# Down projection of the last two blocks: plain tiles before, quads of seven half-size products after

## The chip, the cores and the metric

One Trainium2 chip, one of its cores. The metric is the device time of one execution in microseconds (us), median of several runs. The engines are TensorE (PE, with its weight loads PEld), VectorE (DVE), ScalarE (ACT), GpSimd (POOL) and SyncE (SP, whose queue issues all DMAs here).

## The reference

One step of a one-layer hybrid decoder (width 1024) on 2048 prompt tokens and 8x8 sample tokens, 2112 columns in all. Four recurrent mixers (RWKV-7, GLA, gated DeltaNet, Mamba-2) work side by side on the projected input; then comes the part that the change touches, the channel mixer and the final norm:

```python
x = x + gt1 * (y @ w_out)
h = rmsnorm(x, norm2_w) * (1 + sc2) + sh2
x = x + gt2 * (jnp.square(jax.nn.relu(h @ w_up)) @ w_down)   # 1024 -> 4096 -> 1024
y = rmsnorm(x, final_norm_w)
```
All in float32. The kernel holds activations transposed: features on the 128 partitions, tokens on the free axis.

## The kernel before, in words

**Exactness.** Each float32 operand is split into a rounded part `hi` and the rest `lo`, and `mm3` (L111 to 119) forms a product by three matmuls (hi*hi, hi*lo, lo*hi; lines L117, L118, L119) for each slice of 128 of the inner dimension. A weight tile of 128x512 is therefore loaded (`wr`), cast on ACT (`wh`) and subtracted on DVE or POOL (`wl`): `wload` (L92), or `split` (L361), which takes turns between POOL and DVE when no engine is named.

**Stages.** The input projection runs in four passes, with the mixers beside it. Then the tokens go through the channel mixer in blocks, `F_BLOCKS` (L26): two small ones (352 and 360 columns) and two of two tiles of 350 each, the "last two blocks". `F_out` (L321) transposes the mixers' output, multiplies by w_out and writes the residual x to DRAM (`x2`); it is called for the next block in the last step of a small block (L2200 to 2206).

**Up projection of the last two blocks.** It goes by quads: two row tiles of 128 by two column tiles of 350, the inner dimension in two halves of 512. Such a 2x2 product by blocks is made with seven products instead of eight. `forms_x` (L368) makes the seven right factors from the normed input once per block (x2 and x3, in the slots x0 to x13 and z0 to z13; a slot is 128x1400, and a factor takes two, hi and lo). `forms_w` (L415) makes the seven left factors for each quad: four loads of 128x512, three sums on POOL and one on DVE (L428), seven splits (L366). `quad` (L449) runs the seven products, twelve matmuls each, over three PSUM banks, and after each product `read` takes the bank's running sum. `up_quad` (L463) adds, applies relu and square, and stores four hidden tiles of 128x350 to DRAM (L2246, `fd<-r`). Block 2 alone goes through 12 of the 16 quads (`SOLO`), F_out of block 3's second tile stands behind the first of them, then four quads serve both blocks, and then 12 serve block 3 alone. The steps of block 3's forms_x are emitted one per quad in between.

**Down projection of the last two blocks.** Both together, as four column tiles, in eight steps of 512 hidden features. `hidden` (L509) reloads a step's four hidden tiles (128x1400) from DRAM through four raw slots and splits them; `F_down2` (L520) goes over eight row tiles of 128 and four column tiles, twelve matmuls each, and adds each result times its gate into the residual (`gated_add`, L314). The last step runs in three parts (two tiles, one, one), each with the ending `F_end2` (L531): sum of squares, rstd, scaling (L545), store.

**What sets the order.** The program is emitted in the order told; a planner then orders each engine's instructions by priority and by its own estimate of times, and keeps that order fixed. Each engine, and SP's queue of DMAs, works in order. A tile with a tag has a fixed number of buffers, and a new one waits until the old one's last reader is done.

Of the kernel before, what the change touches and what calls it, by code (L numbers as in the profile page):

```python
# [28 lines left out]
WR, WH, WL = 4, 3, 3  # L29
# [7 lines left out]
class Dense:  # L37
    def __init__(self, es, tc, io):
# [6 lines left out]
        self.uid = self.lo_i = self.mod_i = 0  # L45
        self.held = self.aux = self.w_dma = self.xalloc = self.dsh = None
# [321 lines left out]
    def forms_x(self, bi, rs, slot, out, tmp):  # L368
# [10 lines left out]
        for k in range(4):  # L379
            q = {}  # L380
            for name, kk, t0, r in (("12", k, tb, rb), ("11", k, ta, ra), ("22", k + 4, tb, rb), ("21", k + 4, ta, ra)):
                t = q[name] = tmp(k, False)[:, :n]
                self.xget(t, self.x2, kk, t0, n)
                nc.vector.scalar_tensor_tensor(out=t, in0=t, scalar=self.A2[:, kk, 0:1], in1=r[:, :n], op0=ALU.mult, op1=ALU.mult)

            def sub(a, b, eng, o=None):
                o = tmp(k, True)[:, :n] if o is None else o
                eng.tensor_tensor(out=o, in0=a, in1=b, op=ALU.subtract)
                return o
# [10 lines left out]
            t1 = sub(q["12"], q["11"], nc.gpsimd)  # L400
            put(0, q["11"], s0)
            put(2, q["21"], s1)
            yield
            u = sub(q["22"], t1, nc.vector)
# [10 lines left out]
    def forms_w(self, srcs, wide):  # L415

        nc = self.nc
        ws = lambda: self.sb.tile([128, 512], F32, tag="ws", name=self.n("ws"), bufs=4)[:, :wide]
        raw = {}
        for i, h in ((0, 0), (1, 0), (1, 1), (0, 1)):  # L420
            t = ws() if (i, h) == (1, 0) else self.wp.tile([128, 512], F32, tag="wr", name=self.n("wr"), bufs=WR)[:, :wide]
            nc.sync.dma_start(t, srcs[i][:, h * wide : h * wide + wide])
            raw[i, h] = t
        a11, a12, a21, a22 = raw[0, 0], raw[0, 1], raw[1, 0], raw[1, 1]

        def comb(a, b, op, out=None):
            o = ws() if out is None else out
            (nc.gpsimd if out is None else nc.vector).tensor_tensor(out=o, in0=a, in1=b, op=op)  # L428
            return o
# [12 lines left out]
        s4 = comb(a12, s2, ALU.subtract)  # L442
        yield parts(a12, nc.vector)
        yield parts(s3, nc.gpsimd)
# [4 lines left out]
    def quad(self, srcs, wide, blocks, read, alt=0):  # L449


        ps = {}
        for i, w in enumerate(self.forms_w(srcs, wide)):
            bank, first = (0, 1, 0, 1, 2, 1, 2)[i], i in (0, 1, 4)
            for b, n, xs in blocks:
                if first:
                    ps[b, bank] = self.psum("de"[(b + alt) % 2])[:, :n]
                p = ps[b, bank]
                hi, lo = xs[i]
                self.mm3(p, w, [(hi[:, k], lo[:, k]) for k in range(wide // 128)], first, True, skip_group_check=True)  # L460
                read(b, i, p)

    def up_quad(self, pair, blocks, tmp, out):  # L463

        nc = self.nc
        held = {}

        def read(b, i, p):
            n = p.shape[1]
            t = lambda tag: tmp(b, tag)[:, :n]  # L470
            if i == 0:
                s = held[b, "s"] = t("s")
                nc.scalar.copy(s, p)
                return
            if i in (1, 3):
                u = held[b, i] = t("u" if i == 1 else "v")
                nc.vector.tensor_tensor(out=u, in0=p, in1=held[b, "s"], op=ALU.add)  # L477
                return
            r = t("r")
            if i == 2:  # L480
                nc.scalar.activation(r, p, AF.Relu)
            else:
                nc.vector.tensor_tensor(out=r, in0=p, in1=held[b, {4: 3, 5: "s", 6: 1}[i]], op=ALU.add)
                nc.scalar.activation(r, r, AF.Relu)
            nc.scalar.activation(r, r, AF.Square)
            row, col = {2: (0, 0), 4: (1, 1), 5: (1, 0), 6: (0, 1)}[i]
            out(2 * pair + row, 2 * b + col, r)

        self.quad([self.io["w_up"][2 * pair + i] for i in range(2)], 512, blocks, read, pair % 2 if len(blocks) == 1 else 0)
# [19 lines left out]
    def hidden(self, f_d, cc, take, raws, parts):  # L509

        f = []
        for j in range(4):
            raw = take(raws)
            self.nc.sync.dma_start(raw.bitcast(F32), f_d[cc * 4 + j])
            hi, lo = take(parts), take(parts)
            self.split(hi, lo, raw.bitcast(F32))
            f.append((hi, lo))
        return f

    def F_down2(self, tiles, f, acc, cc):  # L520

        for c2 in range(4):
            w = self.wload(self.io["w_down"][cc, c2])
            for ci in range(2):
                ct = c2 * 2 + ci
                for i, (o, n) in enumerate(tiles):
                    ps = self.psum("de"[i % 2])[:, :n]
                    self.mm3(ps, w[ci], [(fh[:, o : o + n], fl[:, o : o + n]) for fh, fl in f])
                    self.gated_add(acc[ct][:, o : o + n], ps, 40, ct, 0, n)

    def F_end2(self, acc, t0, o, n):  # L531

        nc = self.nc
        s = self.d2("ssum", 2)
        for ct in range(KT):
            self.sumsq(s[:, :n], acc[ct][:, o : o + n], ct == 0)
        r = self.rstd_bc(s, n)
        tail = t0 + n == NT
        for ct in range(KT):
            a = acc[ct][:, o : o + n]  # L540
# [1495 lines left out]
D2_BUFS = 6  # L2036
SOLO = 12
# [22 lines left out]
def build(tc, io):  # L2060
    nc = tc.nc
    with ExitStack() as es:
# [129 lines left out]
        pl = es.enter_context(tc.tile_pool(name="left", bufs=1, side="left", reuse_waits="tile"))  # L2192
        hs = first["hs"]
        for bi in range(SMALL):
# [5 lines left out]
            for cc in range(8):  # L2200
                f = K.F_up(bi, hs, lambda j: (f0[:, 0, j], f0[:, 1, j]), cc)
                if cc == 7:
                    rs = K.F_out(bi + 1, yload, ("a0", "a1"))
                    if final:
                        rs2 = K.F_out(bi + 2, yload, ("a0", "a1"), slice(0, 1), salloc=lambda: pl.tile([128, BIG], F32, tag="ssum", name=K.n("ssum"), bufs=2))
# [8 lines left out]
        W2 = 4 * BIG  # L2214
        slots = {}

        def slot(pool, tag):
            slots[tag] = pool.tile([128, W2], F32R, tag=tag, name=K.n("sl"), bufs=1)
            return slots[tag]

        def y_act(tags, n):
            t = [slot(pr, tag).rearrange("p (k n) -> p k n", k=4) for tag in tags]
            return [HalfTiles(t[:2]), HalfTiles(t[2:])]

        def yall(t0, m):
            t = slot(pr, yslots.pop(0)).bitcast(F32)[:, :1024]
            yget(t, t0, m, slice(0, 1024))
            return t

        yslots = ["z6", "z7", "z8"]  # L2230
        x2, x3 = [], []
        small = lambda tag, bufs: pl.tile([128, BIG], F32, tag=tag, name=K.n(tag), bufs=bufs)
        first_x = lambda k, second: (small("s2", 3) if second else pl.tile([128, 512], F32, tag="ws", name=K.n("xw"), bufs=4)) if k % 2 else K.d2()
        for _ in K.forms_x(two[0], rs, lambda i: slot(pl, f"x{i}"), x2, first_x):
            pass
# [6 lines left out]
        f_d = [K.dram.tile([128, W2], F32, name=f"fd{i}") for i in range(32)]  # L2242
        T0 = F_BLOCKS[two[0]][0][0]
        K.xalloc = lambda: pr.tile([128, BIG], F32, tag="r2", name=K.n("r2"), bufs=3)
        tmp = lambda b, tag: K.xalloc() if tag == "r" else K.d2() if b else small("s2", 3)
        fout = lambda ct, q, r: nc.sync.dma_start(f_d[ct][:, q * BIG : q * BIG + BIG], r)  # L2246
        late = list(range(16 - SOLO, 16))
        for i, p in enumerate(late):
            K.up_quad(p, [(0, BIG, x2)], tmp, fout)
            if i == 0:  # L2250
                rs2 += K.F_out(two[1], yload, ["z0", "z2", "z3", "z4"], slice(1, 2), act=y_act, yall=yall)
                mod = K.forms_x(two[1], rs2, lambda i: slot(pr, f"z{i}"), x3, lambda k, second: K.d2())
            else:
                next(mod)
        for _ in mod:
            pass
        for p in range(16 - SOLO):
            K.up_quad(p, [(0, BIG, x2), (1, BIG, x3)], tmp, fout)
        for p in late:
            K.up_quad(p, [(1, BIG, x3)], tmp, fout)  # L2260
        raws = [f"x{i}" for i in range(4)]
        free = [f"x{i}" for i in range(4, 12)] + [f"z{i}" for i in range(6, 14)]
        acc = []
# [137 lines left out]
```

## Time and profile before

| | us |
|---|---|
| median of 3 runs | 3460.47 |
| lowest and highest | 3449.18 and 3468.5 |
| the profiled execution | 3459.12 |
| its span, first to last instruction | 3457.2 |
| TensorE busy in the span | 3250.1 |
| up stage of the last two blocks | about 2410 to 2944 |
| down stage of the last two blocks | about 2944 to 3441 |

The profile is of one execution. Its page gives busy times by engine, 40 equal slices of the span, DMA rates and groups of instructions by source line ("L119"). Further answers from the trace give the busy times in chosen stretches of time, waits with what ended them, and single instructions in order of time. Matmuls are pipelined: a matmul's shown duration (about 325 ns for 350 columns) is about twice the distance between two of them. PEclk is the share of TensorE's clock that was granted.

### The profile page before, as it was taken

To read this page: it belongs to the slowest core of one execution; us is meant where nothing else is said; L and a number is where in the kernel's file an instruction comes from. 1 tells how busy PE (TensorE), PEld (TensorE's weight loads), DVE (VectorE), ACT (ScalarE), POOL (GpSimd) and SP (SyncE) were. 2 spreads that over 40 slices of the span, in tenths; PEclk is the share of its full clock that TensorE was granted. 3 is DMA by queue.
4 is the path that set the end of the run, shared out by engine and by line. 5 is a ranking of instruction groups with operands and counts; after the bars stand their busy time and mean duration, and the time that the engine had idled before them with its cause. 6 is when DMAs were issued, how large, how long until landed. Compare 5 with 4: busy or idle time off the path is not lost. (4 is left out here: it accounts for less than half of the span.)

```text
span 3457.2 us, 62414 instructions
## 1 busy us (share of the span) xinstructions
PE 3250.1 (94%) x22902; PEld 2966.7 (86%) x22902; DVE 2280.3 (66%) x4728; ACT 1472.2 (43%) x3054; POOL 1390.2 (40%) x1290
## 2 busy tenths in 40 slices
PE   8999999899999998999989999987789999999997
PEld 5779887898998887988878988877689999999997
DVE  3437555956767778879889869867484355445446
ACT  3443423434344454454454554444355566111113
POOL 2333334524335346346346346245375365212112
PEclk9999999899999999999988999988899999999999
DMA  9863334423235564343343333354444455322213
GB/s 307 257 184 114 91 96 133 131 83 111 93 96 132 145 141 137 104 119 101 114 136 121 98 117 96 119 162 156 147 128 125 133 168 168 119 69 93 75 34 122
DMA packets 350395, 438.61 MB, mean 127 GB/s; under 512 B 100627, under 2 KB 228395, under 8 KB 350089
## 3 DMA queue, kind: packets, MB, share of 16 engines
q1 hardware_dynamic: 350088, 434.63, 41.4%
q8 instruction: 180, 2.95, 0.4%
q14 instruction: 127, 1.03, 0.1%
HBM read 346.75 MB, written 87.74 MB: 126 GB/s over the span
## 5 line engine op out<-in xcount | busy, mean ns | idle before, releaser
L102 POOL TENSOR_TENSOR wl<-wr,wh 128x512 fp32r<-128x512 f32 x344 | 476.1, 1385 | 1105.7 <-ACT wh L100 989.5
L119 PE MATMUL psd<-a,wl 128*128 128x360 f32 (+3 forms) x2368 | 805.1, 341 | 33.1 <-DVE wl L102 27.0
L117 PE MATMUL psd<-a,wh 128*128 128x360 f32 (+3 forms) x2368 | 801.0, 339 | 7.8 <-ACT wh L100 3.9
L118 PE MATMUL psd<-a,wh 128*128 128x360 f32 (+3 forms) x2368 | 801.9, 339 | 5.6 <-DVE a L257 2.5
L100 ACT CAST wh<-wr 128x512 fp32r<-128x512 f32 x688 | 422.1, 617 | 875.7 <-PE psd L118 423.7
L119 PEld LDWEIGHTS psd<-a,wl 128*128 128x128 f32 x2368 | 463.5, 196 | 75.1 <-DVE wl L102 34.7
L117 PEld LDWEIGHTS psd<-a,wh 128*128 128x128 f32 x2368 | 463.6, 196 | 33.3 <-issue 9.8
L118 PEld LDWEIGHTS psd<-a,wh 128*128 128x128 f32 x2368 | 463.6, 196 | 22.5 <-issue 10.2
L102 DVE TENSOR_TENSOR wl<-wr,wh 128x512 fp32r<-128x512 f32 x344 | 282.4, 821 | 152.2 <-ACT wh L100 139.4
L117 PE MATMUL psd<-sl,wh 128*128 128x350 f32 x992 | 325.0, 328 | 15.3 <-DVE sl L314 3.9
L117 PE MATMUL pse<-sl,wh 128*128 128x350 f32 x992 | 323.6, 326 | 8.1 <-DVE s L477 6.2
L119 PE MATMUL pse<-sl,wl 128*128 128x350 f32 x992 | 321.8, 326 | 1.7 <-DVE wl L366 0.6
L118 PE MATMUL psd<-sl,wh 128*128 128x350 f32 x992 | 323.2, 326 | 0.0
L118 PE MATMUL pse<-sl,wh 128*128 128x350 f32 x992 | 321.4, 324 | 0.0
L119 PE MATMUL psd<-sl,wl 128*128 128x350 f32 x992 | 321.1, 325 | 0.0
L117 PEld LDWEIGHTS psd<-sl,wh 128*128 128x128 f32 x992 | 189.2, 191 | 17.5 <-issue 8.8
L117 PEld LDWEIGHTS pse<-sl,wh 128*128 128x128 f32 x992 | 188.0, 190 | 9.7 <-ACT wh L362 6.2
L871 DVE SCALAR_TENSOR_TENSOR t<-u,cw,t 128x256 f32<-128x256 f32 x288 | 188.9, 691 | 4.9 <-ACT t L867 3.9
L119 PEld LDWEIGHTS pse<-sl,wl 128*128 128x128 f32 x992 | 187.7, 189 | 3.1 <-DVE wl L366 1.2
L118 PEld LDWEIGHTS psd<-sl,wh 128*128 128x128 f32 x992 | 190.0, 192 | 0.0
L119 PEld LDWEIGHTS psd<-sl,wl 128*128 128x128 f32 x992 | 189.3, 191 | 0.6 <-DVE wl L366 0.3
L118 PEld LDWEIGHTS pse<-sl,wh 128*128 128x128 f32 x992 | 188.6, 190 | 0.1
(630 smaller groups left out, 6327.0 us busy)
## 6 DMA issues: line engine op xcount, KB each, us to landing
wr<-w_in SPq DMA_DIRECT2D x256, 256.0 KB
wr<-w_up SPq DMA_DIRECT2D x212, 256.0 KB
wr<-w_down SPq DMA_DIRECT2D x208, 256.0 KB
ada<-ada_w SPq DMA_DIRECT2D x96, 256.0 KB
wr<-w_out SPq DMA_DIRECT2D x96, 256.0 KB
u<-uo SPq DMA_DIRECT2D x128, 180.0 KB
fd<-r SPq DMA_DIRECT2D x128, 175.0 KB
sl<-fd SPq DMA_DIRECT2D x32, 700.0 KB
```

The costliest lines, as they stand in the source:

```text
L100: nc.scalar.copy(hi, raw)
L102: self.lo_eng[self.lo_i % len(self.lo_eng)].tensor_tensor(out=lo, in0=raw, in1=hi.bitcast(F32), op=ALU.subtract)
L117: nc.tensor.matmul(ps, lhsT=lh, rhs=xh, start=first and i == 0, stop=False, **kw)
L118: nc.tensor.matmul(ps, lhsT=lh, rhs=xl, start=False, stop=False, **kw)
L119: nc.tensor.matmul(ps, lhsT=ll, rhs=xh, start=False, stop=last and i == len(ks) - 1, **kw)
L871: nc.vector.scalar_tensor_tensor(out=y[:, q], in0=uv[:, q, i : i + n], scalar=w(i), in1=y[:, q], op0=ALU.mult, op1=ALU.add)
```

## The change

The down projection of each of the last two blocks goes by quads too: 2 blocks, in each 4 steps of 1024 hidden features (two halves of 512), in each 4 pairs of row tiles. The seven right factors of a step, sums and differences of hidden tiles, are made in the up stage by `up_quad` and stored to DRAM in place of the four hidden tiles (28 factors per block, 128x1400 each). `form_f` loads a factor through one of two raw slots and splits it in four pieces of 350; the first step's seven are formed during block 3's up quads 5 to 11, a later step's two in the third quad and five in the fourth quad of the step before. `down_quad` adds each product into the residual, with product 0 summed in a tile of its own (`e0`) until the last step. The down stage may put two of five weight parts into slots of its own (`wmore`), so that five are held rather than three.

With it come: each up quad serves one block (16 + 16 quads); in `forms_w` the sum s2 moves from POOL to DVE and is made in place; `forms_x` makes t1 in place and takes all its tiles from one tag with five buffers (`D2_BUFS` 6 to 5), for block 2 where odd steps had other tags; three of the four F_out tiles of the last blocks load rows of 1024 columns at once (one before); F_out of block 3's second tile stands behind three up quads (`OUT3_AT`); the sums of squares are taken as each row tile is finished, and `F_end2` runs once per column tile at the end of each block.

```diff
         def parts(x, eng=None):
-            hi = self.wp.tile([128, 512], F32R, tag="wh", name=self.n("wh"), bufs=WH)[:, :wide]
-            lo = self.wp.tile([128, 512], F32R, tag="wl", name=self.n("wl"), bufs=WL)[:, :wide]
+            self.part_i += 1
+            if self.wmore is not None and self.part_i % 5 in (1, 3):
+                t = self.wmore()
+                hi, lo = t[:, 0:512], t[:, 512:1024]
+            else:
+                hi = self.wp.tile([128, 512], F32R, tag="wh", name=self.n("wh"), bufs=WH)
+                lo = self.wp.tile([128, 512], F32R, tag="wl", name=self.n("wl"), bufs=WL)
             self.split(hi, lo, x, eng)
             return hi, lo
 
         yield parts(a11, nc.vector)
-        s1 = comb(a21, a22, ALU.add)
-        s2 = comb(s1, a11, ALU.subtract)
+        s1 = comb(ws(), a21, a22, ALU.add)
+        s3 = comb(a21, a11, a21, ALU.subtract, nc.vector)
+        s2 = comb(a11, s1, a11, ALU.subtract, nc.vector)
         yield parts(s2, nc.gpsimd)
-        s3 = comb(a11, a21, ALU.subtract, a21)
-        s4 = comb(a12, s2, ALU.subtract)
         yield parts(a12, nc.vector)
+        s4 = comb(a12, a12, s2, ALU.subtract)
         yield parts(s3, nc.gpsimd)
         yield parts(s1, nc.vector)
         yield parts(a22, nc.gpsimd)
         yield parts(s4, nc.vector)
...
+    def up_quad(self, src, xs, n, alt, tmp, out):
...
+            else:
+                add(t["u2"], p, t["u2"])
+                act(t["u2"])
+                add(new("t1"), t["u2"], t["r2"], nc.vector, ALU.subtract)
+                out(4, t["t1"])
+                add(new("t2"), t["v2"], t["t1"], nc.vector, ALU.subtract)
+                out(1, t["t2"])
+                add(t["u2"], t["v2"], t["u2"], nc.gpsimd, ALU.subtract)
+                out(3, t["u2"])
+                add(new("t4"), t["s2"], t["t2"], nc.vector, ALU.subtract)
+                out(5, t["t4"])
...
+    def form_f(self, f_d, raw, part):
+
+        hi, lo = part(), part()
+        self.nc.sync.dma_start(raw, f_d)
+        h = raw.shape[1] // 4
+        for o in range(0, 4 * h, h):
+            self.split(hi[:, o : o + h], lo[:, o : o + h], raw[:, o : o + h])
+        return [x.rearrange("p (k n) -> p k n", k=4) for x in (hi, lo)]
+
+    def down_quad(self, src, xs, n, alt, p, acc, e0, first, last, between):
...
+        def gated(row, col, x):
+            a = acc[row, col]
+            nc.vector.scalar_tensor_tensor(out=a, in0=x, scalar=self.mod[:, 40 + 2 * p + row, 0:1], in1=a, op0=ALU.mult, op1=ALU.add)
...
+        def add(i, ps):
+            if i == 0:
                 if first:
+                    nc.scalar.copy(e0, ps)
+                else:
+                    nc.vector.tensor_tensor(out=e0, in0=ps, in1=e0, op=ALU.add)
+                if last:
+                    for row, col in ((0, 1), (1, 0), (1, 1)):
+                        gated(row, col, e0)
                 return
+            gated(*{1: (0, 1), 2: (0, 0), 3: (1, 1), 4: (1, 1), 5: (1, 0), 6: (0, 1)}[i], ps)
...
+        parts = [f"x{i}" for i in range(10)] + [f"z{i}" for i in range(8)]
+        raws = ["x10", "x11"]
+        more = ["z8", "z9"]
+        pairs = ["x12", "x13", "z10", "z11", "z12", "z13", "x12", "x13"]
...
+        mod, nxt = None, []
+        for b in range(2):
+            for p in range(16):
+                c, k = p // 4, p % 4
+                K.up_quad(lambda i, h: io["w_up"][8 * c + 4 * i + k][:, h * 512 : h * 512 + 512], (x2, x3)[b], BIG, p % 2, utmp,
+                          lambda i, t: nc.sync.dma_start(f_d[b][c][i][:, k * BIG : k * BIG + BIG], t))
+                if b == 0 and p == OUT3_AT:
+                    rs2 += K.F_out(two[1], yload, ["z0", "z2", "z3", "z4"], slice(1, 2), act=y_act, yall=yall("z", (6, 7, 8)))
+                    mod = K.forms_x(two[1], rs2, lambda i: slot(f"z{i}"), x3, lambda k: K.d2())
+                elif mod:
+                    next(mod, None)
+                if b == 1 and 5 <= p < 12:
+                    nxt.append(K.form_f(f_d[0][0][len(nxt)], take(raws).bitcast(F32), lambda: take(parts)))
...
+            for c in range(4):
+                cur, nxt = nxt, []
+                at = (4 * b + c + 1) // 4, (c + 1) % 4
+                for p in range(4):
+                    def between(i):
+                        if at[0] < 2 and ((p == 2 and i < 2) or (p == 3 and 1 <= i < 6)):
+                            nxt.append(K.form_f(f_d[at[0]][at[1]][len(nxt)], take(raws).bitcast(F32), lambda: take(parts)))
+
+                    K.down_quad(lambda i, h: io["w_down"][2 * c + h, p][:, i * 512 : i * 512 + 512], cur, BIG, p % 2, p, acc[p], e0[p], c == 0, c == 3, between)
+                    if c == 3:
+                        for row in range(2):
+                            for col in range(2):
+                                K.sumsq(sums[col][:, :BIG], acc[p][row, col], p == row == 0)
+            for col, (t0, n) in enumerate(tiles2):
+                K.F_end2([acc[ct // 2][ct % 2, col] for ct in range(KT)], sums[col], t0, n, b == 1)
```

More of the change, by code (lines that the diff above doesn't have):

```diff
@@ L447, in forms_w, with quad @@
         yield parts(s4, nc.vector)
-    def quad(self, srcs, wide, blocks, read, alt=0):
+    def quad(self, src, xs, n, alt, read):
         ps = {}
-        for i, w in enumerate(self.forms_w(srcs, wide)):
+        for i, w in enumerate(self.forms_w(src)):
             bank, first = (0, 1, 0, 1, 2, 1, 2)[i], i in (0, 1, 4)
-            for b, n, xs in blocks:
-                if first:
[L457 to L473, printed above, removed]
-                return
[L475 to L489, printed above, removed]
+            if first:
+                ps[bank] = self.psum("de"[alt])[:, :n]
@@ L507, in F_up, with F_end2 @@
         return f
[L509 to L531, printed above, removed]
+    def F_end2(self, acc, s, t0, n, tail):
         nc = self.nc
-        s = self.d2("ssum", 2)
+        r = self.rstd_bc(s, n)
         for ct in range(KT):
[L536 to L540, printed above, removed]
+            a = acc[ct]
             if tail and ct in (2, 5):
@@ L2035 @@
 MOD_AT = 26
-D2_BUFS = 6
-SOLO = 12
+OUT3_AT = 2
+D2_BUFS = 5
 SMALL = sum(len(b) == 1 for b in F_BLOCKS)
@@ L2192, in build, with yall, load @@
         pl = es.enter_context(tc.tile_pool(name="left", bufs=1, side="left", reuse_waits="tile"))
+        W2 = 4 * BIG
+        slot = lambda tag: (pl if tag[0] == "x" else pr).tile([128, W2], F32R, tag=tag, name=K.n("sl"), bufs=1)
+        small = lambda tag, bufs: pl.tile([128, BIG], F32, tag=tag, name=K.n(tag), bufs=bufs)
+        def yall(side, free):
+            free = iter(free)
+            def load(t0, m):
+                t = slot(f"{side}{next(free)}").bitcast(F32)[:, :1024]
+                yget(t, t0, m, slice(0, 1024))
+                return t
+            return load
         hs = first["hs"]
@@ L2213, in build @@
         two = (SMALL, SMALL + 1)
[L2214 to L2219, printed above, removed]
+        UT = dict(s2=2, u2=2, v2=1, r2=1, t1=1, t2=1, t4=1)
+        utmp = lambda tag: (pl if tag in ("s2", "u2") else pr).tile([128, BIG], F32, tag=tag, name=K.n(tag), bufs=UT[tag])
         def y_act(tags, n):
-            t = [slot(pr, tag).rearrange("p (k n) -> p k n", k=4) for tag in tags]
+            t = [slot(tag).rearrange("p (k n) -> p k n", k=4) for tag in tags]
             return [HalfTiles(t[:2]), HalfTiles(t[2:])]
[L2225 to L2230, printed above, removed]
         x2, x3 = [], []
-        small = lambda tag, bufs: pl.tile([128, BIG], F32, tag=tag, name=K.n(tag), bufs=bufs)
-        first_x = lambda k, second: (small("s2", 3) if second else pl.tile([128, 512], F32, tag="ws", name=K.n("xw"), bufs=4)) if k % 2 else K.d2()
-        for _ in K.forms_x(two[0], rs, lambda i: slot(pl, f"x{i}"), x2, first_x):
+        for _ in K.forms_x(two[0], rs, lambda i: slot(f"x{i}"), x2, lambda k: K.d2()):
             pass
@@ L2241, in build @@
         K.phase(pl, BIG, D2_BUFS, None, lo)
[L2242 to L2263, printed above, removed]
-        for ct, tag in enumerate(["x12", "x13"] + [f"z{i}" for i in range(6)]):
-            t = slot(pl if tag[0] == "x" else pr, tag).bitcast(F32)
-            nc.sync.dma_start(t, K.x2[:, ct, T0:])
-            acc.append(t)
-        turn = {id(raws): 0, id(free): 0}
+        K.xalloc = K.d2
+        f_d = [[[K.dram.tile([128, W2], F32, name=f"fd{b}_{i}_{c}") for i in range(7)] for c in range(4)] for b in range(2)]
+        parts = [f"x{i}" for i in range(10)] + [f"z{i}" for i in range(8)]
+        raws = ["x10", "x11"]
+        more = ["z8", "z9"]
+        pairs = ["x12", "x13", "z10", "z11", "z12", "z13", "x12", "x13"]
+        e0s = ["s2", "s2", "u2", "u2", "v2", "r2", "t1", "t2"]
+        turn = {id(parts): 0, id(raws): 0, id(more): 0}
         def take(tags):
@@ L2272, in take @@
             turn[id(tags)] += 1
-            return slot(pl if tag[0] == "x" else pr, tag)
-        tiles4 = [(i * BIG, BIG) for i in range(4)]
-        f = K.hidden(f_d, 0, take, raws, free)
-        for cc in range(8):
-            cur = f
-            if cc < 7:
-                f = K.hidden(f_d, cc + 1, take, raws, free)
-                K.F_down2(tiles4, cur, acc, cc)
-        for part in (tiles4[:2], tiles4[2:3], tiles4[3:]):
-            K.F_down2(part, cur, acc, 7)
-            for o, n in part:
-                K.F_end2(acc, T0 + o, o, n)
+            return slot(tag)
@@ new lines, in build @@
+        for b in range(2):
+            tiles2 = F_BLOCKS[two[b]]
+            acc, e0 = [], []
+            for p in range(4):
+                t = slot(pairs[4 * b + p]).bitcast(F32).rearrange("p (q n) -> p q n", q=4)
+                a = {}
+                for q in range(4):
+                    row, col = q // 2, q % 2
+                    a[row, col] = t[:, q]
+                    nc.sync.dma_start(t[:, q], K.x2[:, 2 * p + row, tiles2[col][0] : tiles2[col][0] + BIG])
+                acc.append(a)
+                e0.append(utmp(e0s[4 * b + p])[:, :BIG])
+            sums = [K.d2("ssum", 2) for _ in range(2)]
+            K.wmore = lambda: take(more)
+            for c in range(4):
+                cur, nxt = nxt, []
+                at = (4 * b + c + 1) // 4, (c + 1) % 4
+                for p in range(4):
+                    def between(i):
[8 more added lines that the diff above has]
+                K.F_end2([acc[ct // 2][ct % 2, col] for ct in range(KT)], sums[col], t0, n, b == 1)
```

75 lines of the change are left out of this document (56 added, 19 removed).

## The prediction

> **What bounds the kernel now.** I read the page's first part, a table of stages for the whole core, and the same table for one matmul line, since a mean over all stages would hide where TensorE has gaps.
>
> ```profile
> PE 3250.1 (94%) x22902; PEld 2966.7 (86%) x22902; DVE 2280.3 (66%) x4728; ACT 1472.2 (43%) x3054; POOL 1390.2 (40%) x1290
> ```
> ```profile
> core 0: us, PE busy (x) PEld busy (x) DVE busy (x) ACT busy (x) POOL busy (x), PEclk, DMA share, GB/s
> 2410.00:2460.00 50.00, 29.00 (x145) 25.85 (x144) 21.21 (x32) 14.57 (x29) 10.47 (x8) 0.69 0.37 122
> 2500.00:2560.00 60.00, 44.78 (x238) 42.47 (x237) 57.68 (x71) 34.39 (x72) 42.59 (x32) 0.89 0.39 115
> 2560.00:2672.00 112.00, 112.00 (x697) 111.69 (x696) 58.06 (x82) 69.12 (x133) 68.45 (x51) 1.00 0.44 133
> 2782.00:2944.00 162.00, 161.34 (x1005) 161.09 (x1004) 88.28 (x122) 101.88 (x190) 97.53 (x69) 1.00 0.50 164
> 2944.00:3395.00 451.00, 451.00 (x2800) 451.00 (x2799) 206.37 (x282) 72.41 (x94) 93.89 (x44) 1.00 0.22 74
> ```
> ```profile
> 2410.00:2460.00 50.00, 12.78 (x36) 7.81 (x36) 0.69 0.37 122
> 2500.00:2560.00 60.00, 26.42 (x78) 16.29 (x78) 0.89 0.39 115
> 3395.00:3441.40 46.40, 25.36 (x76) 14.81 (x76) 0.96 0.42 136
> 3441.40:3457.20 15.80, 0.00 (x0) 0.00 (x0) 0.66 0.47 166
> ```
> From 2560 to 3395 us TensorE has no gap and the full clock: up stage until 2944, then down. There 451/2800 = 0.161 us passes per matmul of 350 columns, and only fewer matmuls or new gaps can move the time. Elsewhere it has gaps: the second table is L119, one matmul in three, so 2410 to 2460 holds 3x36 = 108 of them, 17.4 us of work in 50, and 2500 to 2560 234, 37.7 in 60.
>
> In that window VectorE (DVE) is busy 57.7 of 60. Why shows in the timeline:
>
> ```profile
> 2541.84 1.57 POOL L428 TENSOR_TENSOR ws<-ws,wr 128x512 f32<-128x512 f32 x1
> 2542.18 1.78 DVE L366 TENSOR_TENSOR wl<-ws,wh 128x512 fp32r<-128x512 f32 x1
> 2543.37 1.38 POOL L366 TENSOR_TENSOR sl<-d,sl 128x350 fp32r<-128x350 f32 x1
> 2543.89 1.25 DVE L397 SCALAR_TENSOR_TENSOR sl<-d,dsh,sl 128x350 fp32r<-128x350 f32 x1
> ```
> ```profile
> L366 POOL TENSOR_TENSOR wl<-ws,wh x56: 1279/1292/1657, 2413.9 to 2925.6; 128x512 fp32r<-128x512 f32 x56
> L366 DVE TENSOR_TENSOR wl<-ws,wh x56: 673/693/2748, 2418.5 to 2931.7; 128x512 fp32r<-128x512 f32 x56
> ```
> ```profile
> 2514.27 0.57 DVE L384 SCALAR_TENSOR_TENSOR d<-d,A,rstd 128x350 f32<-128x350 f32 x1
> 2519.00 0.92 POOL L366 TENSOR_TENSOR sl<-d,sl 128x350 fp32r<-128x350 f32 x1
> 2526.14 0.51 DVE L366 TENSOR_TENSOR sl<-d,sl 128x350 fp32r<-128x350 f32 x1
> ```
> ```profile
> L483 DVE TENSOR_TENSOR r<-psd,s x30: 504/523/525, 2429.9 to 2772.6; 128x350 f32<-128x350 f32 x30
> ```
> A DVE subtraction of 512 takes 0.68 us undisturbed; behind a GpSimd (POOL) one it took 1.78 and ended 0.55 us after it; the next POOL one then ended 0.79 us after DVE's. They take turns. L483, which reads PSUM, never exceeds 0.525. So DVE operations with both inputs in SBUF share one resource, "the pair", with POOL's. What can it carry? The first and last of twelve DVE and six POOL groups in 2500 to 2560:
>
> ```profile
> L397 DVE SCALAR_TENSOR_TENSOR sl<-d,mod,sl 128x350 fp32r<-128x350 f32 x16 | 15.9, 997 | 0.2 <-ACT sl L396 0.2
> ...
> L477 DVE TENSOR_TENSOR s<-psd,s 128x350 f32<-128x350 f32 x2 | 1.0, 510 | 0.0
> ```
> ```profile
> L388 POOL TENSOR_TENSOR d<-d,d 128x350 f32<-128x350 f32 x12 | 14.5, 1214 | 4.4 <-DVE sl L397 2.3 <-DVE d L384 2.1
> ...
> L366 POOL TENSOR_TENSOR sl<-d,sl 128x350 fp32r<-128x350 f32 x3 | 3.4, 1131 | 0.0
> ```
> All groups together: POOL 17 of 512 and 15 of 350; DVE 14 of 512, 35 scalar and 8 plain ones of 350, and 14 that read PSUM. By the undisturbed durations the pair's share is 17x1.28 + 15x0.92 + 14x0.68 + 35x0.57 + 8x0.51 = 69.1 us, done in 60: pair work costs 0.87 of its undisturbed sum.
>
> The Trainium skill, "SBUF — State Buffer", section "Who interferes with whom", says the loser of this pair blocks for the whole instruction. Read literally, the factor is 1.0, the window would have needed 69 us, and the sum below would be some 40 us higher; the trace has the blocking, with 0.87.
>
> **The change, part by part.** The sum goes against the profiled execution, 3459.1 us (span 3457.2), 1.4 below the median 3460.5.
>
> *Fewer matmuls.* Down before: 8 steps x 8 row tiles x 4 column tiles x 12 = 3072. After: 2 blocks x 4 x 4 quads of 7 products x 12 = 2688. 384x0.161 = **-61.8 us**.
>
> *The end.* The last step ran in three parts, each with its own ending: 3395 to 3441.4 holds 3x76 = 228 matmuls, 36.7 us, so 9.7 were lost. One part remains; I take 8 back. After the last matmul stand 15.8 us of squares, rstd, scaling and stores; both column tiles now end there: between 0 and 8x0.57 = 4.6 more, I take 2. Together **-6**.
>
> *Pair work of one weight quad.* After: POOL 3 subtractions and 2 sums, DVE 4 and 2, all of 512: 5x1.28 + 6x0.68 = 10.5, x0.87 = 9.1 us beside 84 matmuls, 13.5 us. (Before, up stage: 6 and 5, 9.6 us, and 2782 to 2944 ran without gaps.)
>
> *Up stage.* The four quads that served both blocks become eight; their preparation hides like the others'. Each quad gains three DVE and one POOL subtraction of 350, (3x0.51+0.92)x0.87 = 2.1: 11.2 of 13.5. Seven factors are formed in block 1's quads; each costs two POOL and two DVE pieces, (2x0.92+2x0.51)x0.87 = 2.5 us, and two of the seven must wait until z0 to z3 are free, at the end. The other five exceed the 2.3 us of slack by little: 0 to 9 us, I take 5. Block 1's own inputs (forms_x) already cost 60-37.7 = 22 us in 2500 to 2560; with the fuller pair I add 5 (0 to 15). Block 0's inputs now use five buffers for five tiles per step, where odd steps had buffers of their own, so each of four steps waits for its loads (0.7 MB at the page's highest rate, 307 GB/s, 2.3 us): +8 (0 to 15). Against this, F_out of the last tile moves behind two more quads:
>
> ```profile
> PE pst L337 <- DMA sl<-yd: 15.9, 2, 11.5
> ```
> Those 15.9 us of waiting get 27 us of cover, if SyncE (SP) issues the loads early: -15 (-20 to 0). SP's queue also takes seven factor stores per quad for four, behind which weight loads stand; the page's rate has room:
>
> ```profile
> GB/s 307 257 184 114 91 96 133 131 83 111 93 96 132 145 141 137 104 119 101 114 136 121 98 117 96 119 162 156 147 128 125 133 168 168 119 69 93 75 34 122
> ```
> Per quad 1 MB of weights and 1.2 MB of stores in 13.5 us are 167 GB/s. Up stage together **+3** (-20 to +35).
>
> *Down stage.* Before, cheap 350-column reads and few splits left the pair half idle. The reads stay (six or seven a quad, one input in PSUM, no pair). New are the weight quads, 4x9.1 per step, and seven factors, 7x2.5: 53.9 us of pair work in 4x13.5 = 54.1 of TensorE. On average it just fits, but five factors are formed in the fourth quad and two in the third: 14.1 and 21.6 us against 13.5 each, 8.7 over. Five weight buffers let four products (4x1.3 = 5.2 us) be ready beforehand, and a factor is needed some eight products after its slot is free. So a step stalls between 0 (factors yield to weights) and 8.7 us (factors first); halfway, 4.5, is also near 8.7-5.2. Seven steps form factors: **+31.5** (0 to 61). At the change of blocks come 16 sums of squares and 16 scalings on DVE, (16x0.51+16x0.57)x0.87 = 15, of which idle pair time in early quads takes a third: **+10** (0 to 15); block 1's later accumulators also wait for block 0's stores there.
>
> ScalarE: 7x0.62 casts plus five factors at 1.36 are 11.1 us in the fourth quad, below 13.5:
>
> ```profile
> L362 ACT CAST sl<-sl 128x1400 fp32r<-128x1400 f32 x24 | 31.5, 1359 | 35.0 <-PE pse L119 35.0
> L100 ACT CAST wh<-wr 128x512 fp32r<-128x512 f32 x47 | 29.1, 620 | 269.2 <-PE pse L118 269.2
> ```
> Sum: 3459.1-61.8-6+3+31.5+10 = **3436 us**.
>
> **Rivals.** *The pair is hidden.* If factors yield to weights, steps do not stall and the up stage gains: 3459-62-8-10+15 = 3394, rounded up to 3400. For it: 2560 to 2944 ran gapless at 70% of the pair. Against: 100% in the down stage.
>
> *SP's queue becomes the bound, slower than before.* Factors load through two raw slots:
>
> ```profile
> SPq L514 <- DVE sl L366: 64.6, 13, 7.6
> ```
> Today a factor load waits 5.0 us (64.6/13) at SP until a slot is split, harmless with weights far ahead. Five such loads in the fourth quad are 25 us with the next weights behind them in the queue, against one quad, 13.5 us, of weights loaded ahead: 11.5 us of stall per step in place of 4.5, 7x7 = 49 more, 3485. It loses against before from 4.5+23/7 = 7.8 us per step. For it: five loads and one quad of weights, 4.5 MB in 13.5 us, are 333 GB/s, above the page's highest slice. Against: the load order is planned, and loads can slip into the next quad.
>
> *The pair at factor 1.0.* A step needs 4x10.5+7x2.86 = 62.0 us against 54.1, a stall of 7.9, and the up stage some 16 more: 3436+7x3.4+16 = 3476, no change. Against: the window above.
>
> **How the numbers follow.** A measurement of this kernel tells about 0.5% (17 us) from no change: below 3443 is faster, above 3478 slower. Forecast 0.45 (0.32 of it below 3443), hidden pair 0.25, SP's queue 0.18 (0.02 of it below 3478), factor 1.0 0.12 (a sixth above 3478). Faster 0.57, same 0.13+0.02+0.10 = 0.25, slower 0.18. The range, 3385 to 3485, reaches to both outer cases; the forecast's own is 3412 to 3460.
>
> **What would show it.** PE falls to 22518 instructions. In the down stage TensorE is gapless in the first two quads of a step and waits in the fourth or right after it for wl, a weight split by POOL or DVE. DVE operations of 512 there average well over 0.68 us. The 15.9 us wait for yd is gone. If the down stage is gapless, the pair theory fails; if SP waits for slots while TensorE waits for weight loads (wr by DMA), the queue was it. Gaps before 2944 above 35 us over today's would put the fault in the up stage.

## The result and the profile after

The changed kernel takes 3544.9 us (median of 4 runs, 3532.6 to 3551.6) against 3461.7 before (median of 4): the ratio is 1.024, 95% interval 1.022 to 1.026. It is slower by 2.4%, outside the range of 3385 to 3485. The profiled execution after took 3549.8 us, 90.7 more than the one of before.

The page's first part, the changed kernel:

```profile
PE 3246.9 (92%) x22518; PEld 2938.6 (83%) x22518; DVE 2613.6 (74%) x5106; ACT 1617.5 (46%) x3428; POOL 1669.0 (47%) x1532
```
The 384 matmuls are gone (22902 to 22518), but TensorE is busy nearly as long as before. DVE does 378 operations more and is busy 333 us longer, which is 0.88 us for each, where none of the kinds added takes more than 0.7 undisturbed. Stages of the changed kernel:

```profile
2550.00:2650.00 100.00, 81.74 (x432) 77.92 (x431) 88.70 (x113) 55.40 (x112) 64.15 (x48) 0.88 0.44 139
2650.00:2750.00 100.00, 93.31 (x561) 89.81 (x560) 74.51 (x95) 55.73 (x109) 50.96 (x40) 1.00 0.47 151
2750.00:2800.00 50.00, 41.63 (x220) 39.10 (x219) 36.42 (x46) 27.93 (x60) 32.03 (x26) 0.90 0.76 247
2800.00:2900.00 100.00, 93.24 (x557) 88.86 (x556) 75.47 (x95) 56.06 (x108) 53.85 (x42) 1.00 0.50 158
```
```profile
3020.00:3528.00 508.00, 460.22 (x2687) 449.12 (x2686) 427.80 (x566) 223.04 (x456) 343.53 (x256) 0.95 0.43 144
```
Where the kernel before passed 6.2 matmuls per us (1005 in 162 us), the plain up quads of 2650 to 2750 and 2800 to 2900 now pass 5.6. The inputs of the last block (2550 to 2650) and the five factors of the first down step, which the planner drew together in 2750 to 2800, slow it to 4.3 and 4.4. The down stage passes its 2687 matmuls in 508 us, where 0.161 us each would make 433.

Its start and end are seen by the first and last read of a product:

```profile
L534 ACT COPY s<-psd x1: 427/427/427, 3020.6 to 3020.6; 128x350 f32<-128x350 f32 x1
```
```profile
L525 DVE SCALAR_TENSOR_TENSOR sl<-pse,mod,sl x96: 566/574/584, 3036.8 to 3528.1; 128x350 f32<-128x350 f32 x96
```
and, of the kernel before:

```profile
L314 DVE SCALAR_TENSOR_TENSOR sl<-psd,mod,sl x136: 562/582/585, 2941.5 to 3443.7; 128x350 f32<-128x350 f32 x136
```
The first read moved from 2941.5 to 3020.6: the stages before it lost 79 us. From there to the last read it is 507.5 after 502.2, and from the last read to the end 19.6 after 13.5. 79.1+5.3+6.1 is the 90.5 by which the span grew. So most of the loss arose ahead of the down stage, in the up stage above all, and the down stage gave all its 61.8 us away again.

What one quad looks like, in lines picked from the changed kernel's timeline at 2836 us, after product 6 of one up quad and at product 1 of the next:

```profile
2836.09 1.57 POOL L366 TENSOR_TENSOR wl<-ws,wh 128x512 fp32r<-128x512 f32 x1
2836.55 1.49 DVE L469 TENSOR_TENSOR t<-v,t 128x350 f32<-128x350 f32 x1
2837.62 1.22 POOL L469 TENSOR_TENSOR u<-v,u 128x350 f32<-128x350 f32 x1
2838.07 1.15 DVE L469 TENSOR_TENSOR t<-s,t 128x350 f32<-128x350 f32 x1
2839.14 0.51 DVE L469 TENSOR_TENSOR u<-psd,s 128x350 f32<-128x350 f32 x1
2839.71 0.43 PE L117 MATMUL psd<-sl,wh 128*128 128x350 f32 x1 [0.37 <-DVE u L469]
```
The two subtractions `t` take 1.49 and 1.15 us for 0.51, and each ends about 0.4 us after the POOL operation that ran beside it. The read of product 1 (u from psd), which needs no pair, stands behind them in DVE's queue, and product 3 may not use that PSUM bank before it: TensorE waits 0.37 us. Nothing here is overfull; DVE is busy 75% and the pair, by the prediction's count, 83%. Nor is it one case. The waits of TensorE from 2650 to 2750 (total, times, longest, in us):

```profile
PE pse L117 <- DVE v L469: 2.1, 2, 1.8
PE psd L117 <- DVE v L469: 1.7, 4, 0.8
PE pse L117 <- DVE u L469: 1.2, 3, 0.4
PE psd L117 <- DVE u L469: 1.2, 3, 0.4
PE pse L117 <- ACT wh L362: 0.5, 1, 0.5
```
All but the last are for reads of a bank (u and v of L469), 6.2 of 6.7 us; from 2410 to 3020 such waits make 32 of 75.

### The profile page after: what moved, and what is told of

The parts are those of the page before. It is cut to its first block, busy times and chain, and to the rows that moved or that the text cites. A ratio compares the mean times of both kernels' runs of the same rounds, so it can differ in the third digit from the quotient of the medians.

```text
span 3547.7 us, 63317 instructions
## 1 busy us (share of the span) xinstructions
PE 3246.9 (92%) x22518; PEld 2938.6 (83%) x22518; DVE 2613.6 (74%) x5106; ACT 1617.5 (46%) x3428; POOL 1669.0 (47%) x1532
## 4 chain that ended last, share of the span: by engine, by line
PE 57%; DVE 24%; DMA 7%; issue 6%; ACT 3%; POOL 3%; SPq 1%; DVEq 0%; POOLq 0%; ACTq 0%
PE psd L117 12%; PE psd L119 12%; PE psd L118 12%; DVE t L899 2%; PE pse L117 2%; DVE sl L366 2%; PE pse L119 2%; PE pse L118 2%; PE psm L173 2%; DVE t L469 2%; DMA wr<-w_up 2%; DVE wl L102 2%; DVE sl L525 2%; DVE wl L366 1%; DVE Xt L718 1%
## 5 line engine op out<-in xcount | busy, mean ns | idle before, releaser
L119 PE MATMUL psd<-a,wl 128*128 128x360 f32 (+3 forms) x2368 | 803.0, 340 | 33.1 <-DVE wl L102 28.5
L102 POOL TENSOR_TENSOR wl<-wr,wh 128x512 fp32r<-128x512 f32 x304 | 421.9, 1389 | 757.0 <-ACT wh L100 658.5
L100 ACT CAST wh<-wr 128x512 fp32r<-128x512 f32 x608 | 372.1, 616 | 508.6 <-PE psd L118 399.9
L119 PEld LDWEIGHTS psd<-a,wl 128*128 128x128 f32 x2368 | 462.1, 195 | 74.4 <-DVE wl L102 36.0
L102 DVE TENSOR_TENSOR wl<-wr,wh 128x512 fp32r<-128x512 f32 x304 | 239.6, 788 | 140.8 <-ACT wh L100 133.4
L117 PE MATMUL pse<-sl,wh 128*128 128x350 f32 x780 | 263.9, 338 | 28.0 <-DVE v L469 9.0
L119 PE MATMUL pse<-sl,wl 128*128 128x350 f32 x780 | 257.4, 333 | 12.9 <-DVE wl L366 9.9
L117 PE MATMUL psd<-sl,wh 128*128 128x350 f32 x716 | 241.5, 337 | 21.4 <-DVE v L469 9.5
L118 PE MATMUL pse<-sl,wh 128*128 128x350 f32 x780 | 258.6, 332 | 0.0
L362 ACT CAST wh<-wr 128x512 fp32r<-128x512 f32 x256 | 157.2, 618 | 214.5 <-PE pse L118 79.4
L119 PE MATMUL psd<-sl,wl 128*128 128x350 f32 x716 | 235.3, 332 | 12.0 <-DVE wl L366 9.5
L118 PE MATMUL psd<-sl,wh 128*128 128x350 f32 x716 | 237.1, 331 | 0.0
L366 POOL TENSOR_TENSOR wl<-wr,wh 128x512 fp32r<-128x512 f32 x102 | 141.9, 1391 | 163.3 <-ACT wh L362 150.3
L117 PEld LDWEIGHTS pse<-sl,wh 128*128 128x128 f32 x780 | 152.6, 196 | 39.3 <-ACT wh L362 13.8
L119 PE MATMUL psd<-f,wl 128*128 128x352 f32 (+1 forms) x512 | 173.9, 344 | 6.0 <-DVE wl L102 5.5
L117 PE MATMUL psd<-f,wh 128*128 128x352 f32 (+1 forms) x512 | 173.2, 346 | 6.6 <-DVE acc L314 4.1
L118 PE MATMUL psd<-f,wh 128*128 128x352 f32 (+1 forms) x512 | 173.2, 340 | 2.5 <-DVE f L559 2.5
```

The lines of the kernel that those rows point to most:

```text
L100: nc.scalar.copy(hi, raw)
L102: self.lo_eng[self.lo_i % len(self.lo_eng)].tensor_tensor(out=lo, in0=raw, in1=hi.bitcast(F32), op=ALU.subtract)
L117: nc.tensor.matmul(ps, lhsT=lh, rhs=xh, start=first and i == 0, stop=False, **kw)
L118: nc.tensor.matmul(ps, lhsT=lh, rhs=xl, start=False, stop=False, **kw)
L119: nc.tensor.matmul(ps, lhsT=ll, rhs=xh, start=False, stop=last and i == len(ks) - 1, **kw)
L362: self.nc.scalar.copy(hi, x)
```

## The experiments

The theory after the result: the pair of DVE and POOL, but not by its capacity. A pair operation on DVE lasts until POOL's is done, and DVE, working in order, holds up the PSUM reads behind it, on which the next product waits. Its rivals: SP's queue and the factor loads; DVE's own work; the order of the weight sums. The runs without rounds are one execution each. The first four are from one chip, where the kernel before took 3453.1 beside them; the others are from another, where it took 3472.6 beside the next four and 3458.6 to 3481.3 in 13 later executions. A difference of total times below some 15 us between single runs therefore says little, and one across the two chips is uncertain by as much.

| run | us | first to last gated read, down stage | its length |
|---|---|---|---|
| changed kernel | 3549.8 | 3020.9 to 3528.1 | 507.2 |
| e1_nosubs | 3514.1 | 2990.9 to 3492.6 | 501.7 |
| e2_nolo | 3487.9 | 3017.8 to 3466.2 | 448.4 |
| e3_dve | 3469.6 | 2981.2 to 3447.8 | 466.6 |
| e4_noload | 3558.0 | 3029.1 to 3536.5 | 507.4 |
| e5_yload | 3442.2 | 2951.5 to 3420.0 | 468.5 |
| e6_spread | 3434.4 | 2942.7 to 3412.4 | 469.7 |
| e7_pool01 | 3455.7 | 2948.4 to 3434.6 | 486.2 |
| e10_yload_only | 3529.4 | 2998.7 to 3508.0 | 509.3 |

**e1_nosubs**, from the changed kernel:

```diff
-                add(new("t1"), t["u2"], t["r2"], nc.vector, ALU.subtract)
-                out(4, t["t1"])
-                add(new("t2"), t["v2"], t["t1"], nc.vector, ALU.subtract)
-                out(1, t["t2"])
-                add(t["u2"], t["v2"], t["u2"], nc.gpsimd, ALU.subtract)
+                out(4, t["u2"])
+                out(1, t["v2"])
                 out(3, t["u2"])
-                add(new("t4"), t["s2"], t["t2"], nc.vector, ALU.subtract)
-                out(5, t["t4"])
+                out(5, t["s2"])
```


> The changed kernel without the four subtractions per up quad that form the sums of hidden tiles (three on DVE, one on POOL); the seven stores stay and send the undifferenced tiles. Theory, the DVE and POOL pair with DVE working in order: the burst of subtractions behind product 6 makes the next quad's reads late, some 1.3 us per quad, so 32 quads give back about 40 us: total near 3505, and 2650 to 2950 runs without gaps again (over 103 matmuls of each line per 50 us where the changed kernel has 94). Rival, the stores in SP's queue or the fewer buffers of the new temporaries: those stay, so the time stays within 10 us of 3545.

36 us less than the profiled changed kernel, 31 less than its median; the down stage begins 30 us earlier and is 5.5 us shorter. The four subtractions are a cost, near the 40 expected. But 2650 to 2950 reached 98 to 101 matmuls of each line per 50 us (88 where the factors are formed), not 103: about half of what a quad lost stayed. The temporaries t1, t2 and t4 go with the subtractions, so a part of the gain could be theirs; e3_dve keeps them.

**e2_nolo**:

```diff
-        hi, lo = part(), part()
+        hi, _ = part(), part()
...
-            self.split(hi[:, o : o + h], lo[:, o : o + h], raw[:, o : o + h])
-        return [x.rearrange("p (k n) -> p k n", k=4) for x in (hi, lo)]
+            self.nc.scalar.copy(hi[:, o : o + h], raw[:, o : o + h])
+        return [x.rearrange("p (k n) -> p k n", k=4) for x in (hi, hi)]
```


> The changed kernel whose formed factors have no lo part: the cast on ACT stays, the 28 subtractions per step on DVE and POOL are left out, and the matmuls read hi twice. Pair theory: the down stage's pair work falls from 53.9 to 36.6 us per step of 54, its stalls (about 70 us) nearly vanish, and the forming of five factors in the up stage costs 14 us less: total near 3470. Rival, the SP queue: loads and waits for raw slots become shorter too, but the DMA traffic stays; it expects half of that at most, near 3510.

3488, between the two figures, and the down stage is 59 us shorter (507 to 448), close to the 433 of its matmuls. The split of the factors makes most of its stalls. That shorter waits of the loads did it is excluded by e4_noload, below. Ahead of the down stage 14 us were expected and 3 came.

**e3_dve**, all on DVE:

```diff
-        def comb(out, a, b, op, eng=nc.gpsimd):
+        def comb(out, a, b, op, eng=nc.vector):
...
-        yield parts(s2, nc.gpsimd)
+        yield parts(s2, nc.vector)
-        yield parts(s3, nc.gpsimd)
+        yield parts(s3, nc.vector)
-        yield parts(a22, nc.gpsimd)
+        yield parts(a22, nc.vector)
...
-                add(t["u2"], t["v2"], t["u2"], nc.gpsimd, ALU.subtract)
+                add(t["u2"], t["v2"], t["u2"], nc.vector, ALU.subtract)
...
-            self.split(hi[:, o : o + h], lo[:, o : o + h], raw[:, o : o + h])
+            self.split(hi[:, o : o + h], lo[:, o : o + h], raw[:, o : o + h], self.nc.vector)
```


> The changed kernel with all pair work of weights, hidden sums and factors on DVE and none of it on POOL (forms_x stays as it is). Pair theory: a subtraction of 512 holds the pair 0.6 us on DVE where POOL holds it 1.1, so a weight quad costs 6.6 us for 9.1, a factor 1.7 for 2.5, and DVE no longer waits for POOL; DVE is then busy some 11 of 13.5 us: total near 3470 to 3490. Rival, DVE as the bound by its own work: more work on the fuller engine makes it slower, above 3570.

3470, 75 us less than the changed kernel's median, at the lower end of what the pair theory gave, while the rival asked for more than 3570. The work is the same; only POOL is out of it. (With POOL's operations go also DVE's waits for their results, 11.1 us for `ws` in the first row of groups below; no run separates the two.) Its stages, in the same columns:

```profile
2650.00:2750.00 100.00, 100.00 (x623) 100.00 (x622) 83.96 (x147) 62.48 (x120) 0.00 (x0) 1.00 0.55 171
2800.00:2900.00 100.00, 100.00 (x624) 100.00 (x623) 84.50 (x148) 61.80 (x119) 0.00 (x0) 1.00 0.55 175
```
```profile
2981.00:3448.00 467.00, 443.29 (x2689) 431.99 (x2688) 431.69 (x814) 222.29 (x452) 3.81 (x4) 1.00 0.47 154
```
The up quads run without a gap again at 84% of DVE, where they did not at 75%. In the down stage DVE does 814 operations in the 432 us in which the changed kernel's did 566 in 428. The groups show why, first three of the changed kernel's DVE (2800 to 2950), then the same three here (2800 to 2900); the last columns are busy time and mean ns, idle time before:

```profile
L427 DVE TENSOR_TENSOR ws<-wr,ws 128x512 f32<-128x512 f32 x11 | 16.8, 1531 | 11.1 <-POOL ws L427 11.1
L469 DVE TENSOR_TENSOR t<-v,t 128x350 f32<-128x350 f32 x10 | 13.5, 1352 | 0.3
L469 DVE TENSOR_TENSOR t<-u,r 128x350 f32<-128x350 f32 x10 | 12.7, 1268 | 5.7 <-ACT u L473 5.7
```
```profile
L427 DVE TENSOR_TENSOR ws<-wr,ws 128x512 f32<-128x512 f32 x8 | 5.5, 684 | 0.0
L469 DVE TENSOR_TENSOR t<-v,t 128x350 f32<-128x350 f32 x7 | 3.6, 518 | 0.0
L469 DVE TENSOR_TENSOR t<-u,r 128x350 f32<-128x350 f32 x7 | 3.6, 517 | 0.0
```

**e4_noload**:

```diff
-        self.nc.sync.dma_start(raw, f_d)
+        if f_d is not None:
+            self.nc.sync.dma_start(raw, f_d)
...
-            nxt.append(K.form_f(f_d[at[0]][at[1]][len(nxt)], take(raws).bitcast(F32), lambda: take(parts)))
+            nxt.append(once())
...
+        def once():
+            i = turn["once"] = turn.get("once", -1) + 1
+            if i < 2:
+                kept.append(take(raws).bitcast(F32))
+            return K.form_f(f_d[0][0][i] if i < 2 else None, kept[i % 2], lambda: take(parts))
```


> The changed kernel that loads two factors only and splits those again for each later factor: 54 of 56 loads of 700 KB and their waits in the SP queue are left out, all splits stay. Rival, the SP queue and DMA: the down stage loses most of its 70 us of stalls, total near 3490. Pair theory: nearly nothing changes, 3530 to 3550.

3558, a little above the 3530 to 3550 of the pair theory, and the down stage is as long to 0.2 us without 54 of the 56 loads. SP's waits are long in the changed kernel (117 us in all at the factor loads there), but leaving those loads out gains nothing. This rival is out.

**e5_yload**, from e3_dve:

```diff
-                    rs = K.F_out(bi + 1, yload, ("a0", "a1"), slice(0, 1))
-                    rs += K.F_out(bi + 1, yload, ("a0", "a1"), slice(1, 2), yall=yall("x", range(6)))
-                    rs2 = K.F_out(bi + 2, yload, ("a0", "a1"), slice(0, 1), salloc=lambda: small("ssum", 2), yall=yall("x", range(6, 12)))
+                    rs = K.F_out(bi + 1, yload, ("a0", "a1"))
+                    rs2 = K.F_out(bi + 2, yload, ("a0", "a1"), slice(0, 1), salloc=lambda: small("ssum", 2))
```


> All pair work on DVE as in the run before, and the F_out tiles of the last two blocks that are made beside the last small block load their rows in pieces of 256 columns again, through buffers of the first phase, as the kernel before does. Theory: the loads of whole rows wait for slots that lie over the mixers' memory, which cost 36 matmuls of each line, 17 us, between 2200 and 2500; the time falls by 10 to 17 us to about 3455. Rival: the new order of the block's forms or its five buffers cost those 17 us; then no change, near 3470.

27 us less, more than expected, and on the chip where the kernel before was the slower; the down stage begins 30 us earlier. The loads of whole rows cost more than the waits that they were to spare.

**e10_yload_only**, the same edit on the changed kernel alone:

> The changed kernel with only the loads of the mixers' rows as before (pieces of 256 columns, buffers of the first phase). If that cost adds to the pair's, as e5_yload against e3_dve says (27 us): near 3518. If the fuller pair hides it: within 10 us of 3545.

3529, 15.5 below the changed kernel's median; the down stage begins 22 us earlier. Between the two expectations. As a total it is one execution, 3 us under the lowest of the changed kernel's four; the earlier start of the down stage, 22 us here and 30 in e5_yload, says that the cost adds to the pair's. Whether a part is hidden by it isn't shown.

**e6_spread**, from e5_yload:

```diff
-                        if at[0] < 2 and ((p == 2 and i < 2) or (p == 3 and 1 <= i < 6)):
+                        if at[0] < 2 and ((p < 2 and i == 3) or (p == 3 and 1 <= i < 6)):
```


> As e5_yload, and of a down step's seven factors the two early ones are formed in the first and second quad in place of the third. Theory: DVE, now the fullest engine of the down stage, is overfull only in the third and fourth quad; moving two factors (1.7 us each) off the third lets weights get ahead: 5 to 20 us less than e5_yload. Rival: the fourth quad alone sets the stall, or the planner forms them in the same place; within 5 us of e5_yload.

8 us less in one execution, but the down stage is no shorter (469.7 after 468.5); the rival holds, and the 8 us arose before it. Timed below, the same kernel is within 3 us of e5_yload.

**e7_pool01**, from e6_spread:

```diff
-        self.quad(src, xs, n, alt, read)
+        self.quad(src, xs, n, alt, read, nc.gpsimd if p < 2 else None)
```
where the last argument takes the three splits and two sums of a weight quad.

> As e6_spread, and POOL does three splits and two sums of each weight quad again in the first and second quad of a down step, where pair work is 9.1 us of 13.5. Pair theory: those quads have room, and DVE is freed of five operations of 0.6 us each, which helps if DVE's own work is the bound there: 0 to 15 us less than e6_spread. If DVE's waits behind POOL cost more than that: 5 to 20 us more.

21 us more, and 10 above the slowest of six executions of e6_spread's kernel (e9_spread5); 16.5 of them arose in the down stage. POOL went back only where the pair had room by the count, 9.1 us of 13.5, and it still cost. This is the clearest sign that capacity was the wrong measure.

**e8_comb**, from the kernel before:

```diff
-        s1 = comb(a21, a22, ALU.add)
-        s2 = comb(s1, a11, ALU.subtract)
+        s1 = comb(ws(), a21, a22, ALU.add)
+        s3 = comb(a21, a11, a21, ALU.subtract, nc.vector)
+        s2 = comb(a11, s1, a11, ALU.subtract, nc.vector)
         yield parts(s2, nc.gpsimd)
-        s3 = comb(a11, a21, ALU.subtract, a21)
-        s4 = comb(a12, s2, ALU.subtract)
         yield parts(a12, nc.vector)
+        s4 = comb(a12, a12, s2, ALU.subtract)
```


> The kernel before with the changed kernel's order and engines of the sums of weight blocks alone (s2 and s3 on DVE behind POOL's s1, s2 and s4 in place), nothing else changed. If the four subtractions on hidden tiles made all of the up stage's loss: within 10 us of 3453. If this order has a part in it (DVE waits for POOL's sum ahead of its reads): 28 quads at 0.4 to 0.8 us each, 10 to 20 us slower.

3470.6, beside 3472.6 of the kernel before on the same chip: no cost to be seen in the time of one execution. The trace shows a small one. Its waits of TensorE from 2650 to 2950:

```profile
PE psd L117 <- DVE d L476: 2.1, 2, 1.8
PE pse L117 <- DVE d L476: 1.5, 1, 1.5
PE psd L117 <- DVE s L476: 1.3, 1, 1.3
```
These 4.9 us are all for reads; the kernel before has one such wait, of 0.7. From 2650 to 2944 it passes 1792 matmuls, the kernel before 1823, which is 5 us, where e1_nosubs passes 1708. So this order is a part of what stayed in e1_nosubs, some 5 of 18 us in that stretch (the forming of five factors is in the 18), and not all of it.

**e11_before_dve**, the kernel before with its sums and splits of up weights on DVE:

> The kernel before with the weight work of its up quads on DVE alone. Pair theory: its up stage had no gaps from 2560 on, so only the stretch from 2500 to 2560, where the inputs of the last block are formed, can gain: 0 to 15 us less, ratio 0.996 to 1. If POOL was a help there (DVE busy 57.7 of 60): slower by 5 us or more.

3455.2 (median of 7) against 3466.8: ratio 0.996, interval 0.995 to 0.998. POOL was no help there either.

**e9_spread5**, the kernel of e6_spread in five rounds:

> The kernel of e6_spread, timed in five rounds against the kernel before. By the single runs (3434 against 3453 and 3473): faster by 0.6 to 1.2%, ratio 0.988 to 0.994. If that was chance: within 0.5% of 1.

3439.4 (median of 6) against 3466.8: ratio 0.992, interval 0.990 to 0.994. With POOL out of the way and the old loads the quads beat the kernel before by 0.8%, and e11_before_dve by some 16 us. Its down stage:

```profile
2949.00:3417.00 468.00, 444.26 (x2689) 432.87 (x2687) 432.60 (x813) 220.85 (x452) 4.06 (x4) 0.99 0.47 155
```
DVE is busy 92% there; 468 less the 433 of its matmuls, 35 of the 61.8 us, are still lost in this stage.

## Why the prediction was wrong

Against the sum, by the profiled executions:

| term | predicted | measured |
|---|---|---|
| 384 matmuls | -61.8 | -61.8 |
| end of the last step and tail | -6 | about -3 |
| up stage and what stands ahead of it | +3 | +79 |
| stalls of the down stage, change of blocks included | +41.5 | about +75 |

*Fewer matmuls* and the *end* held. (The old last step's gaps were worth 7 to 8 us; the tail grew by 4 from the last matmul, to 19.7.)

*The step that failed is "Up stage together +3"*, within it "11.2 of 13.5", from which a plain quad was taken to be hidden. I had found the shared pair and used it as a resource with a capacity, calibrated in the one window where DVE was saturated, and concluded that below 100% nothing is lost. But the pair's cost is a delay: a subtraction on DVE beside POOL's takes 0.7 to 0.85 us more on average (1.24 to 1.53 us where it takes 0.52 to 0.68 alone, in the rows of e3_dve above), what stands behind it on DVE waits, and a PSUM read has only the one product (twelve matmuls, 1.9 us) before its bank is needed again. The kernel before took this at 9.6 of 13.5; with three more subtractions in a row behind product 6 and the new order of the weight sums the changed one did not. e1_nosubs prices the four subtractions at 30 us of the 79, e10_yload_only the row loads at 22. e3_dve gives 40 of the 79 back without removing any work, and e5_yload, which takes back both, begins its down stage at 2951.5, 10 us after the kernel before: POOL's part in the pair work and the row loads account for some 69 of the 79. Of the rest, the inputs of the last block still slow e3_dve (478 matmuls in 2550 to 2650, 432 in the changed kernel, where 621 fit); DVE is busy 92% there, but what part of it is the five buffers wasn't tried. How the half of a quad's loss that e1_nosubs left divides between the seven stores, the buffers of the temporaries that remain and the remaining pair work was tried for the order of the weight sums alone (e8_comb); e3_dve, where it is gone, keeps the stores and the buffers, which points to POOL's work. Whether the shared pair or DVE's waits for POOL's sums weigh more in it stays open.

*The row loads* were not priced at all: I took them as fewer and larger DMAs. *F_out moved behind two quads* brought less than the -15 taken. The changed kernel's waits of TensorE from 2450 to 2560 (total, times, longest):

```profile
PE pst L337 <- DVE sl L341: 8.7, 1, 8.7
...
PE pst L337 <- DMA sl<-yd: 3.3, 1, 3.3
```
Of the 15.9 us for the loads 3.3 are left, but the same transposes now wait 8.7 us once for a split on DVE.

*Down stage*: the place was right (factors, e2_nolo), and so in the main was the wait. The longest of the changed kernel's waits of TensorE from 3026 to 3530 (total, times, longest):

```profile
PE pse L119 <- DVE sl L366: 8.5, 4, 3.2
PE psd L119 <- DVE wl L366: 7.0, 4, 2.7
PE psd L119 <- DVE sl L366: 6.7, 3, 2.8
PE psd L117 <- DVE sl L525: 6.1, 6, 1.8
PE pse L117 <- DVE sl L525: 5.9, 5, 3.0
PE pse L119 <- DVE wl L366: 5.6, 5, 1.9
```
L119 is the matmul that reads a weight's `lo` (in `wl`, or in a slot of `wmore`): 27.8 us are for a weight's split, as forecast, and 12.0 for a read. Counting matmuls from the start of the stage, some 37 of its 47 us of gaps fall into the fourth quad of a step or the first of the next. The size was wrong. About 75 us (509 from its first matmul to its last, less 433) is the sum of both upper ends, 61 and 15. By the same count six of the seven changes of step cost some 7 us each, near the upper 8.7 and not the 4.5 taken, and the one with the change of blocks about 28, where 4.5 and 10 stood. What I hadn't priced is in this piece of the changed kernel's timeline:

```profile
3319.67 1.44 DVE L427 TENSOR_TENSOR wr<-ws,wr 128x512 f32<-128x512 f32 x1
3321.04 3.09 DVE L366 TENSOR_TENSOR sl<-sl,sl 128x350 fp32r<-128x350 f32 x2
3324.05 0.57 DVE L525 SCALAR_TENSOR_TENSOR sl<-psd,mod,sl 128x350 f32<-128x350 f32 x1
```
```profile
3321.89 0.42 PE L117 MATMUL pse<-sl,wh 128*128 128x350 f32 x1 [1.13 <-ACT wh L362]
3324.68 0.66 PE L117 MATMUL psd<-sl,sl 128*128 128x350 f32 x1 [1.68 <-DVE sl L525]
3325.13 0.50 PE L118 MATMUL psd<-sl,sl 128*128 128x350 f32 x1
3325.43 0.49 PE L119 MATMUL psd<-sl,sl 128*128 128x350 f32 x1
...
3330.39 0.48 PE L117 MATMUL pse<-sl,wh 128*128 128x350 f32 x1
3330.68 0.34 PE L118 MATMUL pse<-sl,wh 128*128 128x350 f32 x1
```
```profile
3324.00:3328.00 4.00, 3.32 (x11) 3.32 (x12) 1.72 (x4) 0.00 (x0) 1.28 (x1) 0.50 0.69 247
```
A sum of weights takes 1.44 us on DVE, for about 0.69, and TensorE waits 1.13 us for the cast behind it. Then two pieces of a factor take 3.09 us, for about 0.95; a read stands behind them, and TensorE waits 1.68 us. For the next 6 us its matmuls start 0.29 us apart instead of 0.16, and the granted clock is 0.50. A gap of 2.8 us in all costs some 5.5. Over the down stage the window above says the same: 460.2 us busy for 2687 matmuls, 27.6 more than 433, beside 47.8 us of gaps, and the granted clock of 0.95 over 508 us accounts for about 25 of the 27.6. The forecast priced gaps alone.

The Trainium skill, "TensorE: Matmul & The Clock Gate", Part 1, says that the clock falls to half after a window of about 3.4 us without work. The halving agrees; here four matmuls ran between the two gaps, and the longer one was 1.68 us.

*The rivals.* "SP's queue becomes the bound" named the right side and the wrong cause: e4_noload excludes it. "The pair at factor 1.0" was nearer in cause, but also an argument of capacity, and gave 3476. The sign set beforehand told the place: gaps before 2944 above 35 us over those of the kernel before "would put the fault in the up stage".

## What to carry to other kernels

Where DVE and POOL operations share a resource and DVE also reads PSUM for TensorE, count not only how full the resource is but how late a read or a weight's split can come: the longest run of shared operations that may stand ahead of it in DVE's queue, at disturbed durations, against the time until its bank or its weight is needed. Moving work off the slower sharer can win even when it fills the other engine: here, in plain up quads, DVE at 84% alone ran without gaps, and at 75% beside POOL did not. It has a limit: in the down stage DVE alone, at 92%, still lost 35 us. A saving in matmuls that is paid for in vector operations should be priced with each gap's slow restart included.

## What the runs showed of the hardware that was not expected

A DVE subtraction of 350 that takes 0.52 us alone averages 1.24 to 1.35 beside a POOL busy 54% of the time, 2.5 times as long. And TensorE's clock was halved for about 6 us (0.50 in 3324 to 3328) after waits as short as 1.13 and 1.68 us with four matmuls between them. A wait of that length standing alone did not do it: among the changed kernel's waits of 2650 to 2750, shown above, one is 1.8 us long, and the granted clock of that stretch is 1.00.
